# All tensor sums of the MLPs, their norms and V on VectorE instead of GpSimd, with the adds into y between operand splits and four pairs of operands fetched ahead

## The chip, the cores and the metric

The program runs on one core of one Trainium2 chip. The metric is the device time of one execution in microseconds (us), the median of several runs. A core has five engines that run side by side: PE (TensorE: matmuls, with PEld for its weight loads), DVE (VectorE), ACT (ScalarE), POOL (GpSimd) and SP (SyncE, which here only issues transfers). Each engine runs its instructions in the order in which they stand in its own queue, and an instruction that waits for another engine or for a transfer holds up everything behind it in that queue.

## The reference, cut to what matters

A sequence of 1024 tokens of width 1024, float32, goes through a state-space layer (S5), a norm, an MLP, a norm, then attention, a norm, a second MLP and a last norm:

```
for layer in range(2):
    mix = s5_mixer(x, ...) if layer == 0 else attention(x, k, v, ...)
    x  = layer_norm(ALPHA * x + mix, ...)
    h  = square(relu(x @ w1 + b1))          # 1024 -> 4096
    x  = layer_norm(ALPHA * x + h @ w2 + b2, ...)   # 4096 -> 1024
```

Before layer 1 the shared K and V are made from the output of layer 0 (`v = x @ w_v`). float32 matmuls are done with two reduced-precision halves of each operand: a high part (a cast) and a low part (the operand minus its high part); three products (high x high, high x low, low x high) are summed in PSUM.

## The kernel before

Every MLP matrix product uses Strassen's scheme in Winograd's form on 2 x 2 blocks, so seven products M1 to M7 stand in the place of eight. Their operands are sums of blocks of x, w1, h or w2, and their results are added into more than one block of the output.

**Names.** `split` (L121 to L123) makes the two halves of a 128x512 tile: ACT casts the high part (L122), DVE subtracts for the low part (L123). m0 and m1 are the first matrix of the MLP in layers 0 and 1 (`mlp_up`), d0 and d1 the second (class `Down`). In Down, `d0hM`/`d1hM` is a raw tile of h or of a sum of its blocks (made by mlp_up, kept in DRAM as h_d), `w_d0HM`/`w_d1HM` its two halves; `d0r`/`d1r` is a raw block of w2, `w_d02M`/`w_d12M` the halves of a w2 operand; `d0M`/`d1M` is a PSUM tile, `d0y`/`d1y` the output rows.

**Down.** The contraction over 4096 is cut into 16 pairs of blocks p, four pairs to a chunk, so four chunks. In a chunk the products come in the order M1, M2, M5, M6, M3, M7, M4, each as four units, one for each pair. That is 7 x 4 x 4 = 112 units. A unit is 12 matmuls (four token tiles t, three products each; L1070 to L1072), and the four units of a product add up in four PSUM tiles. There are two sets of these: M1, M6, M7 and M4 use set A, M2, M5 and M3 set C. Where M2 is followed by M5, M7 by M4, or M4 by the next chunk's M1, the next product begins in the very tiles that the last one has filled, so PE may start only when `evict` (L1076 to L1079, on DVE) has added them into y.

The raw block of w2 is turned into the next product's operand in place: `prep` (L1041 to L1061) has one sum on POOL for M5 (L1047), M6 (L1050), M7 (L1055) and M4 (L1060), none for M1, M2 and M3, then a split of h's tile and one of w2's. The loop of `run` goes over the units with operands made LA=3 units ahead and h's tiles loaded LH=2 units before that; behind the last unit of a product stand the four evictions. `load_h`, `load_raw` and `load_y` issue their transfers on SP. `ahead` (L1012 to L1030) runs inside mlp_up: it prepares ALPHA * x + b2 in DRAM (ACT scale L1021, POOL add L1022), and loads and splits the first operands of Down.

**Norms.** `LayerNorm` takes the statistics on DVE (L182 to L190), a power on POOL (L192, 128x1), the centring on ACT (L194), the scale by g on DVE (L203) and the addition of b (L204), the last on POOL but for the second half of the last tile. The norms of the first four token tiles of d0 and d1 run while the last products of Down do. `XOps` makes from the normed x the seven operands of mlp_up: sums (L249 to L256, two on DVE, two on POOL, for a pair of token tiles), transposes on PE, splits.

**V.** `VProject.load` loads and splits w_v; the low part is on POOL for the first eight tiles (L1226), on DVE for the others. It begins during the last units of d0.

The order inside each engine's queue is not quite that of the code: a scheduler moves an instruction forward or back where its dependences and its buffers let it.

Of the kernel before, what the change touches and what calls it, by code (L numbers as in the profile page):

```python
# [9 lines left out]
F32 = mybir.dt.float32  # L10
# [6 lines left out]
P = 128  # L17
# [16 lines left out]
CH = 4  # L34
# [11 lines left out]
def trunk(ctx, tc, A, out):  # L46
# [126 lines left out]
    class LayerNorm:  # L173
# [46 lines left out]
    class XOps:  # L220
# [24 lines left out]
        def more(self, tp_, tag):  # L245

            for n_ in ("T2", "T3", "T4"):
                self.op[n_] = self.two(tp_, tag, n_)

        def sums(self, y, t):  # L250
# [4 lines left out]
            pool.tensor_sub(b0, b1, b0)  # L255
            pool.tensor_sub(a1, t2, a1)  # L256

        def second(self, psp, tag, y, t):
            self.put(psp, tag, "T1", y[t - 4][:, half(0)], t)
            self.put(psp, tag, "B22", y[t][:, half(1)], t)  # L260

        def third(self, psp, tag, y, t):
            self.put(psp, tag, "T2", self.t2.pop(t), t)
# [546 lines left out]
    def mlp_up(l, xo, y_tiles, w1, nm, ypool, tpool, tag, wb, uside, rest, down):  # L810
# [24 lines left out]
        ring = tpool.tile([P, 2, 4, HF], F32, tag=tag, name=f"{nm}ring")  # L835
# [31 lines left out]
        early(1)  # L867
        xo.third(psX, "p", y_tiles, 5)
        rest[1]()
# [9 lines left out]
        early(5)  # L879
        xo.second(psX, "p", y_tiles, 7)  # L880
        early(6)
# [44 lines left out]

        def after(p, m):
            if m in ("M1", "M5", "M6"):
                keep(p, m)
            elif m == "M3":  # L930
                dve.tensor_add(h_new(p, "A21"), tmp[p, "M6"], bank(p, m))
                finish(p, "A21", hs[p, "A21"], 1.0, 0)
            elif m == "M7":
                dve.tensor_add(h_new(p, "A22"), tmp[p, "M5"], bank(p, m))
                finish(p, "A22", hs[p, "A22"], -1.0, 1)
                store(p, "A22", 6)
                dve.tensor_add(h_new(p, "s1"), hs[p, "A21"], hs[p, "A22"])
                store(p, "s1", 1)
            elif m == "M2":
                dve.tensor_add(h_new(p, "A11"), tmp[p, "M1"], tmp[p, "M2"] if p < EA else bank(p, m))  # L940
                finish(p, "A11", hs[p, "A11"], 1.0, 0)
                store(p, "A11", 0)
            else:
# [3 lines left out]
                h_new(p, "s2")  # L947
                dve.scalar_tensor_tensor(hs[p, "s2"], hs[p, "s1"], -1.0, hs[p, "A11"], op0=ALU.mult, op1=ALU.subtract)
                store(p, "s2", 2)
                dve.tensor_add(h_new(p, "s3"), hs[p, "A11"], hs[p, "A21"])  # L950
                store(p, "s3", 4)
                dve.tensor_sub(h_new(p, "s4"), hs[p, "A12"], hs[p, "s2"])
                store(p, "s4", 3)
# [639 lines left out]
```

## Time and profile before

| what | value |
|---|---|
| median of 3 runs | 2513.43 us (2513.2 to 2515.7) |
| the profiled execution | 2512.12 us |
| its span, first to last instruction | 2510.4 us |
| mean granted TensorE clock | 0.971 of full speed |
| PE, DVE, ACT, POOL busy | 92%, 73%, 48%, 35% |
| m0, d0, m1, d1 on PE, from the span's start | 483 to 822, 822 to 1166, 1814 to 2151, 2151 to 2490 us |
| last matmul to the end of the span | 20 us |

Times are microseconds unless marked ns. In a group of instructions, "x112" is the count, "| 94.8, 847 |" the busy time and the mean ns of one, and what follows is the idle time of the engine just ahead of them with what ended most of it. In a timeline each row has the start, the duration, the engine, the line and the operation, and in brackets the engine's idle time before it and who ended it. Rows that a timeline has put together ("x4") have the time of all of them. Matmuls overlap: their starts are 0.23 us apart though each lasts 0.39.

### The profile page before, as it was taken

The numbers are of one execution on the slowest core, as the hardware profiler recorded it, in microseconds if no ns is written. First come the engines' busy times: TensorE is split into PE (matmuls) and PEld (weight loads), VectorE is DVE, ScalarE is ACT, GpSimd is POOL, SyncE is SP. The second block draws the span as 40 slices with busy tenths as digits, with TensorE's granted clock in tenths as the row PEclk, the third lists the DMA queues.
The fourth block names the chain that finished last, engine by engine and source line by source line (L and its number), as shares of the span: only waits on it lengthen the run. The fifth ranks groups of instructions, "written<-read, shape, count | busy, mean of one in ns | idle before, by whom it ended". The sixth has DMA issues, their size and how long they took to land. (4 is left out here: it accounts for less than half of the span.)

```text
span 2510.4 us, 32876 instructions
## 1 busy us (share of the span) xinstructions
PE 2306.3 (92%) x11040; PEld 1882.6 (75%) x11040; DVE 1837.8 (73%) x2652; ACT 1214.0 (48%) x2283; POOL 876.5 (35%) x1012
## 2 busy tenths in 40 slices
PE   9886899989999899998999999988989999899995
PEld 7675787767888777776878788766767888777774
DVE  8788573886665687789159999896777665677787
ACT  5445351365555333434147677663356555344333
POOL 5556340552111431136134444340443112422234
PEclk9989999999999999999999999998999999999998
DMA  4221131365443845435565555555366333654432
GB/s 147 55 72 45 35 126 59 136 245 178 155 147 109 274 153 160 143 92 152 107 153 119 122 128 118 118 139 191 122 206 237 141 141 127 235 193 160 129 103 96
DMA packets 195161, 349.39 MB, mean 139 GB/s; under 512 B 23216, under 2 KB 66224, under 8 KB 194992
## 3 DMA queue, kind: packets, MB, share of 16 engines
q1 hardware_dynamic: 136112, 246.61, 31.1%
q0 software_dynamic: 58880, 100.69, 14.5%
q8 instruction: 87, 1.43, 0.2%
q14 instruction: 82, 0.67, 0.1%
HBM read 212.96 MB, written 100.66 MB: 125 GB/s over the span
## 5 line engine op out<-in xcount | busy, mean ns | idle before, releaser
L1070 PE MATMUL d1M<-w_d12M,w_d1HM 128*128 128x512 f32 x448 | 177.2, 397 | 25.8 <-DVE d1y L1079 19.2
L1070 PE MATMUL d0M<-w_d02M,w_d0HM 128*128 128x512 f32 x448 | 177.7, 397 | 21.3 <-DVE d0y L1079 13.3
L1407 DVE TENSOR_TENSOR_SCAN qq<-qq 128x128 f32<-128x128 f32 (+7 forms) x128 | 174.1, 1362 | 11.5 <-POOL qq L1401 11.2
L1072 PE MATMUL d0M<-w_d02M,w_d0HM 128*128 128x512 f32 x448 | 177.2, 396 | 0.0
L1071 PE MATMUL d0M<-w_d02M,w_d0HM 128*128 128x512 f32 x448 | 176.7, 394 | 0.0
L1072 PE MATMUL d1M<-w_d12M,w_d1HM 128*128 128x512 f32 x448 | 176.4, 394 | 0.0
L1071 PE MATMUL d1M<-w_d12M,w_d1HM 128*128 128x512 f32 x448 | 176.3, 394 | 0.0
L122 ACT CAST w_d0HM<-d0hM 128x512 fp32r<-128x512 f32 x112 | 69.5, 620 | 191.4 <-PE d0M L1072 168.6
L122 ACT CAST w_d1HM<-d1hM 128x512 fp32r<-128x512 f32 x112 | 69.5, 620 | 188.8 <-PE d1M L1072 165.1
L123 DVE TENSOR_TENSOR w_d0HM<-d0hM,w_d0HM 128x512 fp32r<-128x512 f32 x112 | 94.8, 847 | 72.3 <-ACT w_d0HM L122 72.2
L123 DVE TENSOR_TENSOR w_d1HM<-d1hM,w_d1HM 128x512 fp32r<-128x512 f32 x112 | 92.8, 829 | 70.5 <-ACT w_d1HM L122 70.4
L122 ACT CAST wTh<-pt 128x512 fp32r<-128x512 f32 (+1 forms) x192 | 88.2, 486 | 81.3 <-PE pt L1420 80.8
L1420 PE MATMUL pt<-ident,be 128*128 128x128 f32 x576 | 91.7, 284 | 34.0 <-DVE wTl L123 25.3
L1070 PEld LDWEIGHTS d1M<-w_d12M,w_d1HM 128*128 128x128 f32 x448 | 85.1, 190 | 48.2 <-ACT w_d12M L122 21.2
L1070 PEld LDWEIGHTS d0M<-w_d02M,w_d0HM 128*128 128x128 f32 x448 | 85.6, 191 | 43.4 <-ACT w_d02M L122 22.9
L1401 POOL TENSOR_SCALAR_AFFINE_SELECT qq<-qq 128x128 f32<-128x128 f32 x128 | 60.2, 470 | 158.9 <-ACT qq L1398 133.4
L1420 PEld LDWEIGHTS pt<-ident,be 128*128 128x128 f32 x576 | 70.7, 144 | 59.8 <-issue 16.4
L123 DVE TENSOR_TENSOR w_d12M<-d1r,w_d12M 128x512 fp32r<-128x512 f32 x112 | 106.1, 948 | 4.2 <-ACT w_d12M L122 4.2
L123 DVE TENSOR_TENSOR wTl<-pt,wTh 128x512 fp32r<-128x512 f32 (+1 forms) x192 | 99.8, 546 | 11.7 <-ACT wTh L122 11.6
L123 DVE TENSOR_TENSOR w_d02M<-d0r,w_d02M 128x512 fp32r<-128x512 f32 x112 | 102.6, 917 | 4.2 <-ACT w_d02M L122 4.2
L1408 DVE TENSOR_TENSOR be<-be,qq 128x127 f32<-128x127 f32 (+7 forms) x128 | 99.5, 778 | 6.6
L1398 ACT ACTIVATE qq<-pz 128x512 f32<-128x512 f32 (+1 forms) x192 | 97.3, 507 | 10.8 <-DVE be L1408 5.9
(468 smaller groups left out, 7398.1 us busy)
## 6 DMA issues: line engine op xcount, KB each, us to landing
d0hM<-h_d SPq DMA_DIRECT2D x112, 256.0 KB, 2.7
d1hM<-h_d SPq DMA_DIRECT2D x112, 256.0 KB, 2.7
m0ring<-in_w SPq DMA_DIRECT2D x64, 256.0 KB, 3.1
h_d<-m0hs POOLq DMA_DIRECT2D x64, 256.0 KB, 2.8
d0r<-in_w SPq DMA_DIRECT2D x64, 256.0 KB, 3.6
m1ring<-in_w SPq DMA_DIRECT2D x64, 256.0 KB, 3.1
h_d<-m1hs POOLq DMA_DIRECT2D x64, 256.0 KB, 2.6
d1r<-in_w SPq DMA_DIRECT2D x64, 256.0 KB, 3.5
```

Of the source, the lines that this page charges most:

```text
L122: act.copy(hi, src)
L123: dve.tensor_sub(lo, src, hi)
L1070: pe.matmul(ps_, hh[:, tok(t)], wh, start=first, stop=False, skip_group_check=True)
L1071: pe.matmul(ps_, hh[:, tok(t)], wl, start=False, stop=False, skip_group_check=True)
L1072: pe.matmul(ps_, hl[:, tok(t)], wh, start=False, stop=last, skip_group_check=True)
L1398: act.activation(qq[:, s0:s1], pz, AF.Sigmoid, scale=-0.125)
L1401: pool.affine_select(out=tl[:, ns - P:ns], in_=tl[:, ns - P:ns], pattern=[[-1, P]], compare_op=ALU.is_gt, fill=fill, base=0, channel_multi ...
L1407: dve.tensor_tensor_scan(out=rev, data0=rev, data1=rev, initial=1.0, op0=ALU.mult, op1=ALU.bypass)
L1408: dve.tensor_mul(be[:, 0:ns - 1], be[:, 0:ns - 1], qq[:, 1:ns])
L1420: pe.transpose(pt[:, b_], self.be[:, tok(s0 + b_)], ident)
```

## The change

1. The sums of w2's blocks in Down, the adds of b2 in `ahead`, the adds of b in the norms, two of the sums in XOps and the low parts of w_v go from POOL to DVE. The power of the norm, the transfers that POOL issues and the selects in the attention stay on POOL.
2. `prep` is cut into `prep_h` and `prep_w`. At the last unit of a product the order becomes: h's split, two evictions, w2's sum and split, two evictions.
3. Down starts with operands fetched earlier: the ring in which mlp_up keeps raw blocks of w1 is now allocated by XOps (T1 takes its old place), and when mlp_up is through with a part of it, `ahead` loads into it the raw blocks and h's tiles of M1 for pairs 2 and 3 and the four blocks of w2 for M2.
4. In mlp_up the sums s1 to s4 that follow a product are put behind the next product; XOps' T1 transposes come later.
5. In layer 0 the norms of token tiles 2 and 3 move from the end of d0 into V.

```diff
@@ LayerNorm.scale
-                (dve if c.start else pool).tensor_add(y[:, c], y[:, c], self.b[:, c])
+                dve.tensor_add(y[:, c], y[:, c], self.b[:, c])
@@ XOps
-            self.op = {n_: self.two(pl, "act", n_) for n_ in ("B11", "B21", "B22", "T1")}
+            self.op = {n_: self.two(pl, "act", n_) for n_ in ("B11", "B21", "B22")}
+            self.ring = pl.tile([P, 2, 4, HF], F32, tag="act", name=f"{nm}ring")
...
-            pool.tensor_sub(b0, b1, b0)
-            pool.tensor_sub(a1, t2, a1)
+            dve.tensor_sub(b0, b1, b0)
+            dve.tensor_sub(a1, t2, a1)
@@ mlp_up
             prod(p, m, ready.pop((p, m)))
+            if later:
+                later.pop(0)()
             if m == "M5" and p < EA:
-                after(p, "M1")
                 after(p, "M2")
-            down.ahead(i, NSTEPS)
+            if m == "M4" and p + 1 < EA:
+                keep(p + 1, "M1")
+            down.ahead(i, NSTEPS, xo.ring)
             if (p, m) == (0, "M3"):
                 continue
-            after(p, m)
+            later += after(p, m)
@@ Down.ahead
-                    pool.tensor_add(self.yt, self.yt, self.b2[:, half(q % 2)])
+                    dve.tensor_add(self.yt, self.yt, self.b2[:, half(q % 2)])
...
+            if i == n - 7:
+                for q, p in enumerate((2, 3)):
+                    self.load_raw(p, [(0, 0)], to=ring[:, 0, 2 * q])
+                    self.load_h(p, "M1", to=ring[:, 0, 2 * q + 1])
             if i == n - 2:
-                self.ready[0, "M1"] = self.prep(0, "M1")
+                for p in range(4):
+                    self.load_raw(p, [(1, 0)], to=ring[:, 1, p])
+            if i == n - 2:
+                self.ready[0, "M1"] = self.prep_h(0, "M1"), self.prep_w(0, "M1")
@@ Down.prep_w
-                pool.tensor_sub(w, w, r(1, 2))
+                dve.tensor_sub(w, w, r(1, 2))
...
-                pool.tensor_sub(w, r(1, 1), w)
+                dve.tensor_sub(w, r(1, 1), w)
@@ Down.run
-            self.load_h(2, "M1")
-            self.load_raw(2, [(0, 0)])
-            self.load_raw(3, [(0, 0)])
+            self.load_h(0, "M2")
             self.load_y(0, 0)
-            for p in range(CH):
-                self.load_raw(p, self.PARTS[1:2])
...
-                        ready[p, m] = self.prep(p, m)
+                        hw.append(self.prep_h(p, m))
+                        if not end:
+                            hw.append(self.prep_w(p, m))
+                            ready[p, m] = hw
...
-                if q == CH - 1:
-                    for t in range(4):
-                        self.evict(m, t)
+                if end:
+                    self.evict(m, 0)
+                    self.evict(m, 1)
+                    if hw:
+                        c, m_, p = units[i + LA]
+                        hw.append(self.prep_w(p, m_))
+                        ready[p, m_] = hw
...
+                    self.evict(m, 2)
+                    self.evict(m, 3)
@@ VProject.load
-            act.copy(t[:, 0], r)
-            eng.tensor_sub(t[:, 1], r, t[:, 0])
+            split(t[:, 0], t[:, 1], r)
```

In the program as built, 216 tensor sums leave POOL's queue: 128 of w2, 32 of b2, 32 of the norms' b, 16 of XOps and 8 of w_v. PE's and ACT's queues keep their lengths.

The first place is VectorE in d0, second chunk, around the end of M2, where M5 begins in the same PSUM tiles. Before, `w_d0HM` and `w_d02M` are the low halves of operands, and L1079 is the eviction; the sums of w2 stand in POOL's queue:

```order
L123 TENSOR_TENSOR w_d0HM_7635<-d0hM_7587,w_d0HM_7635 128x512
L123 TENSOR_TENSOR w_d02M_7638<-d0r_7353,w_d02M_7638 128x512
L123 TENSOR_TENSOR w_d0HM_7656<-d0hM_7611,w_d0HM_7656 128x512
L123 TENSOR_TENSOR w_d02M_7659<-d0r_7382,w_d02M_7659 128x512
L1079 TENSOR_TENSOR d0y_6781<-d0y_6781,d0M_7595 128x512
L1079 TENSOR_TENSOR d0y_6782<-d0y_6782,d0M_7596 128x512
L1079 TENSOR_TENSOR d0y_6783<-d0y_6783,d0M_7597 128x512
L1079 TENSOR_TENSOR d0y_6784<-d0y_6784,d0M_7598 128x512
L123 TENSOR_TENSOR w_d0HM_7681<-d0hM_7632,w_d0HM_7681 128x512
L123 TENSOR_TENSOR w_d02M_7684<-d0r_7415,w_d02M_7684 128x512
```

Now, at the same place (L1105 is the eviction, L1082 the sum for M6 and L1086 that for M4):

```order
L123 TENSOR_TENSOR w_d0HM_7626<-d0hM_7579,w_d0HM_7626 128x512
L123 TENSOR_TENSOR w_d02M_7630<-d0r_7345,w_d02M_7630 128x512
L1082 TENSOR_TENSOR d0r_7345<-d0r_7345,d0r_7351 128x512
L1086 TENSOR_TENSOR d0r_7347<-d0r_7345,d0r_7347 128x512
L123 TENSOR_TENSOR w_d0HM_7647<-d0hM_7603,w_d0HM_7647 128x512
L1105 TENSOR_TENSOR d0y_6789<-d0y_6789,d0M_7587 128x512
L1105 TENSOR_TENSOR d0y_6790<-d0y_6790,d0M_7588 128x512
L123 TENSOR_TENSOR w_d02M_7665<-d0r_7388,w_d02M_7665 128x512
L1105 TENSOR_TENSOR d0y_6791<-d0y_6791,d0M_7589 128x512
L1105 TENSOR_TENSOR d0y_6792<-d0y_6792,d0M_7590 128x512
L123 TENSOR_TENSOR w_d0HM_7672<-d0hM_7624,w_d0HM_7672 128x512
L123 TENSOR_TENSOR w_d02M_7676<-d0r_7407,w_d02M_7676 128x512
```

Two evictions now stand ahead of the last low half of w2, and two behind it. The sums of M6 and M4 stand behind the last split that reads the block they overwrite, four units or more ahead of the product that uses them; the scheduler has put them there.

The second place is SP's queue where d0 begins. Before, the raw blocks of w1 go to `m0ring`, `r_v` belongs to V, `d0y` is the output's rows:

```order
L842 DMA m0ring<-in_w 128x512 x40
L1223 DMA r_v_9460<-in_w_kv 128x512
L1223 DMA r_v_9465<-in_w_kv 128x512
L1223 DMA r_v_9470<-in_w_kv 128x512
L1038 DMA d0hM_6789<-h_d 128x512
L1083 DMA d0y_6781<-xm_d 128x512
L1083 DMA d0y_6782<-xm_d 128x512
L1083 DMA d0y_6783<-xm_d 128x512
L1083 DMA d0y_6784<-xm_d 128x512
L1038 DMA d0hM_6807<-h_d 128x512
L1038 DMA d0hM_6815<-h_d 128x512
L1038 DMA d0hM_6823<-h_d 128x512
```

and ten loads of `d0r` at L1034 follow. Now the ring is `x1ring`, and L1065 and L1069 are the loads of w2's blocks and of h's tiles:

```order
L843 DMA x1ring<-in_w 128x512 x37
L1065 DMA x1ring<-in_w 128x512 x2
L1069 DMA x1ring<-h_d 128x512 x2
L1065 DMA x1ring<-in_w 128x512 x2
L1259 DMA r_v_9412<-in_w_kv 128x512
L1259 DMA r_v_9417<-in_w_kv 128x512
L1259 DMA r_v_9422<-in_w_kv 128x512
L1065 DMA x1ring<-in_w 128x512 x2
L1069 DMA d0hM_6797<-h_d 128x512
L1109 DMA d0y_6789<-xm_d 128x512
L1109 DMA d0y_6790<-xm_d 128x512
L1109 DMA d0y_6791<-xm_d 128x512
```

Eight of the loads that stood behind y's four rows now stand ahead of them, six of w2's and two of h's.

## Rows read from the trace of the kernel before

**Rows 1.** The page's first part: busy time, share of the span and number of instructions.

```profile
PE 2306.3 (92%) x11040; PEld 1882.6 (75%) x11040; DVE 1837.8 (73%) x2652; ACT 1214.0 (48%) x2283; POOL 876.5 (35%) x1012
```

**Rows 2.** The page's costliest groups: the first matmul of each three in d1 and d0, with PE's idle time before them, and the low halves of w2's operands.

```profile
L1070 PE MATMUL d1M<-w_d12M,w_d1HM 128*128 128x512 f32 x448 | 177.2, 397 | 25.8 <-DVE d1y L1079 19.2
L1070 PE MATMUL d0M<-w_d02M,w_d0HM 128*128 128x512 f32 x448 | 177.7, 397 | 21.3 <-DVE d0y L1079 13.3
...
L123 DVE TENSOR_TENSOR w_d12M<-d1r,w_d12M 128x512 fp32r<-128x512 f32 x112 | 106.1, 948 | 4.2 <-ACT w_d12M L122 4.2
...
L123 DVE TENSOR_TENSOR w_d02M<-d0r,w_d02M 128x512 fp32r<-128x512 f32 x112 | 102.6, 917 | 4.2 <-ACT w_d02M L122 4.2
```

**Rows 3.** PE's waits in d0 (822 to 1166 us): who waited for whom, us in total, times, the longest.

```profile
PE d0M L1070 <- DVE d0y L1079: 13.3, 7, 2.0
PE d0M L1070 <- ACT w_d02M L122: 8.0, 2, 6.7
PE ptd L211 <- POOL d0y L204: 4.5, 3, 1.9
```

and in d1 (2151 to 2490 us):

```profile
PE d1M L1070 <- DVE d1y L1079: 19.2, 8, 6.1
PE d1M L1070 <- ACT w_d12M L122: 6.6, 1, 6.6
```

**Rows 4.** The timeline of d0 around 909 us, where M2 of the first chunk ends and M5 begins in its tiles: DVE and POOL, and the two matmuls on either side of PE's gap. The first row is an operation that no POOL sum overlaps; PE begins M2's last unit at 906.6, 12 matmuls ahead of 909.4.

```profile
902.67 0.69 DVE L123 TENSOR_TENSOR w_d02M<-d0r,w_d02M 128x512 fp32r<-128x512 f32 x1
...
906.85 0.62 ACT L122 CAST w_d0HM<-d0hM 128x512 fp32r<-128x512 f32 x1 [1.58 <-PE d0M L1072]
...
907.50 1.58 DVE L123 TENSOR_TENSOR w_d0HM<-d0hM,w_d0HM 128x512 fp32r<-128x512 f32 x1 [0.33 <-ACT w_d0HM L122]
908.61 1.60 POOL L1055 TENSOR_TENSOR d0r<-d0r,d0r 128x512 f32<-128x512 f32 x1
909.01 1.76 DVE L123 TENSOR_TENSOR w_d02M<-d0r,w_d02M 128x512 fp32r<-128x512 f32 x1
...
910.69 2.47 DVE L1079 TENSOR_TENSOR d0y<-d0y,d0M 128x512 f32<-128x512 f32 x4
...
909.14 0.39 PE L1072 MATMUL d0M<-w_d02M,w_d0HM 128*128 128x512 f32 x1
911.51 0.47 PE L1070 MATMUL d0M<-w_d02M,w_d0HM 128*128 128x512 f32 x1 [1.98 <-DVE d0y L1079]
```

**Rows 5.** Groups of d0's whole stretch (822 to 1166 us): the slowest and the fastest kind of the POOL sums of w2.

```profile
L1060 POOL TENSOR_TENSOR d0r<-d0r,d0r 128x512 f32<-128x512 f32 x16 | 25.3, 1580 | 1.1
...
L1047 POOL TENSOR_TENSOR d0r<-d0r,d0r 128x512 f32<-128x512 f32 x16 | 20.5, 1285 | 142.3 <-DVE w_d02M L123 129.8 <-DMA d0r<-in_w 12.5
```

**Rows 6.** The start of d1: SP's queue, the first cast that had waited for its block, and the matmuls on either side of the gap; the last row is from the chain of waits, the transfer that released the cast.

```profile
2154.23 9.26 SPq L1034 DMA_DIRECT2D d1r<-in_w  x10
...
2162.49 0.62 ACT L122 CAST w_d12M<-d1r 128x512 fp32r<-128x512 f32 x1 [0.81 <-DMA d1r<-in_w]
...
2156.20 0.39 PE L1072 MATMUL d1M<-w_d12M,w_d1HM 128*128 128x512 f32 x1
2163.16 0.80 PE L1070 MATMUL d1M<-w_d12M,w_d1HM 128*128 128x512 f32 x1 [6.57 <-ACT w_d12M L122]
...
2154.23 8.23 DMA d1r<-in_w
```

**Rows 7.** The end of d1, from M7 to M4: POOL, DVE and the matmuls on either side of the gap.

```profile
2467.76 2.92 POOL L204 TENSOR_TENSOR d1y<-d1y,d1b 128x1024 f32<-128x1024 f32 x1 [2.09 <-DVE ved L189]
...
2468.32 2.91 DVE L123 TENSOR_TENSOR w_d12M<-d1r,w_d12M 128x512 fp32r<-128x512 f32 x1
...
2470.72 0.39 PE L1072 MATMUL d1M<-w_d12M,w_d1HM 128*128 128x512 f32 x1
2477.18 0.76 PE L1070 MATMUL d1M<-w_d12M,w_d1HM 128*128 128x512 f32 x1 [6.07 <-DVE d1y L1079]
```

**Rows 8.** The tail of d1, DVE and POOL, from the last evictions to the last addition.

```profile
2487.61 1.29 DVE L1079 TENSOR_TENSOR d1y<-d1y,d1M 128x512 f32<-128x512 f32 x2 [1.50 <-PE d1M L1072]
...
2493.62 3.44 POOL L204 TENSOR_TENSOR d1y<-d1y,d1b 128x1024 f32<-128x1024 f32 x1 [1.33 <-DVE ved L189]
...
2497.02 0.54 POOL L192 TENSOR_TENSOR rsd<-ved,nhalf 128x1 f32<-128x1 f32 x1
...
2497.60 3.35 DVE L203 SCALAR_TENSOR_TENSOR d1y<-d1y,rsd,d1g 128x1024 f32<-128x1024 f32 x1 [2.14 <-POOL rsd L192]
...
2505.36 1.63 DVE L204 TENSOR_TENSOR d1y<-d1y,d1b 128x512 f32<-128x512 f32 x1
```

**Rows 9.** PE's waits in layer 0's projection (381 to 483 us), in V (1166 to 1263 us) and in m1 (1814 to 2151 us), one row of each view.

```profile
PE ptx1T L237 <- DVE y L252: 3.9, 1, 3.9
...
PE pv L118 <- POOL w_v L1226: 1.8, 2, 1.0
...
PE m1A L830 <- DVE m1hA L934: 2.5, 2, 1.6
```

**Rows 10.** Two stretches of the timeline: layer 0's projection (POOL's adds of b beside DVE's splits), and a sum of mlp_up in layer 1.

```profile
468.83 6.13 POOL L204 TENSOR_TENSOR y<-y,sob 128x1024 f32<-128x1024 f32 x2 [1.51 <-DVE y L203]
...
469.86 6.24 DVE L123 TENSOR_TENSOR w_m<-r_m,w_m 128x512 fp32r<-128x512 f32 x3
...
1872.88 3.43 DVE L940 TENSOR_TENSOR m1hA<-m1kM,m1kM 128x512 f32<-128x512 f32 x1
```

More of the change, by code (lines that the diff above doesn't have):

```diff
@@ L867, in mlp_up @@
         early(1)
+        rest[1]()
         xo.third(psX, "p", y_tiles, 5)
-        rest[1]()
         early(2)
@@ L925, in store, with add @@
             pool.dma_start(h_d[p, q], hs[p, n_])
+        def add(p, n_, a, b, op=ALU.add):
+            dve.tensor_tensor(h_new(p, n_), a, b, op=op)
         def after(p, m):
+            later = []
             if m in ("M1", "M5", "M6"):
@@ L957, in mlp_up @@
         steps += [(p, m) for p in range(EA, NP) for m in PROD]
-        ready = {}
+        ready, later = {}, []
         LA = 2
         NSTEPS = len(steps)
+        keep(0, "M1")
         for i in range(-LA, NSTEPS):
@@ L1128, in run @@
             for i in range(-LA, N):
-                if 0 <= i + LA + LH < N and i + LA + LH > 2:
+                if 0 <= i + LA + LH < N and i + LA + LH > CH:
                     self.load_h(units[i + LA + LH][2], units[i + LA + LH][1])
+                end = i >= 0 and units[i][2] % CH == CH - 1
+                hw = []
                 if i + LA < N:
@@ L1133, in run @@
                     if (p, m) not in ready:
-                        ready[p, m] = self.prep(p, m)
-                    if m == "M4" and c + 1 < NP // CH:
+                        hw.append(self.prep_h(p, m))
+                        if not end:
+                            hw.append(self.prep_w(p, m))
+                            ready[p, m] = hw
+                    if m == "M4" and c + 1 < NP // CH and not end:
                         self.load_raw(p + CH, self.PARTS)
@@ L1141, in run @@
                     for _ in range(2):
-                        then.load(0, then.wv, pool)
+                        then.load(0, then.wv)
                 if i < 0:
@@ L1170, in run @@
                             self.unit(p_, m_, ops, (t,), f_, l_)
-                        for f, a in queue.pop(0) if queue else ():
-                            f(a)
                         self.evict(m, t)
@@ L1189, in run @@
                 if fin and m == "M7" and q == CH - 1:
-                    for t in range(4, 8):
+                    for t in range(2 if then else 4, 8):
                         ln(t)
@@ L1195, in run @@
                 for k in range(KD):
-                    then.load(0, then.wv, pool)
+                    then.load(0, then.wv)
                 then.xa = xn
@@ L1216, in begin, with load @@
             self.ws = [[], []]
-        def load(self, n, pl, eng):
+        def load(self, n, pl):
             k = len(self.ws[n])
@@ L1239, in mm @@
                 self.out(n, t, pv)
+            for t in (2, 3):
+                lns[t].stats()
+                lns[t].center()
+            for t in (2, 3):
+                lns[t].scale()
             for t in range(8):
@@ L1245, in run @@
                     lns[4 + t].center()
-                if 1 <= t < 5:
-                    lns[3 + t].scale()
-                if 2 <= t < 6:
+                if t < 6:
+                    if t > 1:
+                        lns[2 + t].scale()
                     trans(t + 2)
-                self.load(1, sl.next(), dve)
+                self.load(1, sl.next())
             for t in range(8):
```

88 lines of the change are left out of this document (48 added, 40 removed).

## The prediction, made before the changed kernel had run

> **What bounds the kernel now.** I read the page's first part, then its costliest groups, PE's waits stage by stage, and timelines of the places where PE stood still. PE is busy for 92% of the span [rows 1], so no edit off PE's path is worth anything, and the most that can be had is PE's idle time. The reader should look at the matmul groups: nearly all of it in the two second MLP matrices stands ahead of the first matmul of a triple, L1070, 25.8 us in d1 and 21.3 in d0 [rows 2]. The waits say for whom: VectorE's evictions, 19.2 and 13.3 us, and the cast of a w2 operand, 6.6 and 8.0 us, nearly all of these in one wait in each layer [rows 3]. So two kinds of wait hold most of what this change could win in Down.
>
> The first is seen around 909 us [rows 4]. M2's last unit starts at 906.6, and its first PSUM tile is complete three matmuls later, at about 907.3. Yet the four evictions start at 910.69, because VectorE is still at two splits of 1.58 and 1.76 us. The same operation takes 0.69 with no GpSimd sum beside it. PE's starts are 2.37 apart there, less a pitch of 0.23, so 2.14 us is lost. The second is a transfer: ten loads of w2 need 9.26 us to be issued, the one that is wanted lands 8.23 us after its issue, and PE's starts at 2156.20 and 2163.16 are 6.96 apart, 6.73 lost [rows 6].
>
> **The change part by part.** The profiled execution took 2512.1 us, 1.3 less than the median; sums are made against it.
>
> *Start of Down.* The operands of M1's four units and the w2 blocks of M2 are fetched inside mlp_up, and eight loads leave the queue ahead of PE's first wants. Nothing that PE needs in the first eight units then waits for the stretch of saturated loads, apart from M2's h tiles. One such gap measures 6.73 [rows 6], the other's wait is as long, 6.7 against 6.6 [rows 3]; after it matmuls take 0.80 in place of 0.39 for a while [rows 6], half a microsecond or so. Both layers: 14 at most. I take -13; if y's rows and h's tiles in the same queue keep half of it, -6; if the queue merely moves the wait to M5, -4.
>
> *Evictions.* d0 has seven waits, d1 seven of the same kind and the 6.1 us one near its end [rows 3]. By 2.14 each, the first of a layer being shorter by some 0.6, that is 14.4 a layer, 28.8 in all. What takes their place? Four evictions back to back take 2.47, one 0.69, so VectorE's pitch is (2.47 - 0.69) / 3 = 0.59, say 0.60 [rows 4]. Count from the start of the last unit: the cast of h starts 0.2 later (906.85 against 906.6) [rows 4], the low half is possible when it ends, at 0.86 and ends its slot at 1.46. The first two evictions then go, done at 2.15 and 2.75, w2's low half has its slot to 3.26, and the other two are done at 3.95 and 4.55. PE wants the four tiles at 2.74, 3.42, 4.10 and 4.79. So nothing waits, but with a margin of 0.15 to 0.7 us only. Left over I put 4 us, for places where VectorE arrives late by a few tenths (14 places by 0.3). Value -24; ends -28.8, and -10 where the last two evictions are late at every place by one slot or more.
>
> This needs VectorE to be on time in spite of its new work: 64 w2 sums a layer. They take GpSimd 1.29 to 1.58 each [rows 5]; VectorE has them for one slot, 0.60. The order places sums for two products behind the splits of M1 and of M5, so these phases hold 8 splits, 8 sums and 4 evictions: 20 x 0.60 = 12.0 against PE's 4 x 2.74 = 10.9. The other five phases hold 12 x 0.60 = 7.2. VectorE falls 1.1 behind twice a chunk, with operands three units ahead, and recovers in the next phase. The stretched splits pay for the rest: their means of 948 and 917 ns against 0.69 [rows 2, 4] are 0.24 x 224 = 54 us that w2's splits alone give back, against 128 x 0.60 = 77 for the sums. The first cover is therefore the lead of three units; if it is gone, each sum costs PE up to 0.60.
>
> *End of d0 and V.* PE waits 4.5 us for GpSimd's adds of b ahead of transposes [rows 3] and 1.8 for w_v's low halves [rows 9], 6.3 together. VectorE takes the adds (two slots each, about 1.2, in place of 2.4 to 2.9), and two of the four norms leave for V, where transposes have to wait for them instead. I take -3; ends -6 (all gone) and +4 (VectorE holds four adds, w_v's splits and V's own splits, 8 x 0.6 more, in one queue).
>
> *End of d1 and the tail.* Between M7 and M4 PE loses 6.2 us (2470.72 to 2477.18) [rows 7]: GpSimd's add takes 2.92 and a split beside it 2.91, where both alone would need 0.69 + 1.2. I count 3.5 left, since the splits and the norms still share VectorE: -2.7. In the tail, an add of 3.44 stands ahead of the power that VectorE then waits for, and VectorE's scale takes 3.35 in place of about 1.3 [rows 8]; but the adds now stand in VectorE's own queue, four of 1.2. From first eviction to last add is 2505.36 + 1.63 - 2487.61 = 19.4 us; I reckon 17, of which 1.2 is lost again because PE ends nearer to the evictions. Together -4; ends -8 and +3.
>
> *Projections and mlp_up.* The longest wait at either projection is 3.9 us for the first sum of XOps [rows 9], itself behind three splits of 6.24 in all that run beside two adds of 6.13 [rows 10]. Alone they would be 1.9 and 2.5. Against that, all four sums of a pair and T1 to T4's transposes hang on VectorE, and 16 adds of b2 a layer (9.6 us) land in a queue whose entries wait in order for their loads. Sums of mlp_up that reach 3.43 beside such an add [rows 10] fall to 0.69. Value -3; ends -14 and +10, as no row shows VectorE with this load at this place.
>
> Sum: -13 - 24 - 3 - 4 - 3 = -47, so 2465 for the profiled execution, **2466 us** against the median.
>
> The trace's slot of 0.60 carries the whole reckoning of VectorE. The Trainium skill (VectorE: DVE Perf Modes, "The TRN2 errata") gives an fp32 add of N elements (N + 151) / 0.96 ns, 691 ns for 512, which agrees with the 0.69 of a single one [rows 4] but not with the slot. By it, if an operation held the engine for all of that, 20 in a phase would need 13.8 against 10.9, and sixteen such phases would be 46 us late, an estimate that leaves 2511. The four evictions in 2.47 speak against it.
>
> **The rivals.**
> 1. *VectorE becomes the bound in M1's and M5's phases, or the last two evictions are late.* For: the surplus of 1.1 us and the margin of 0.15. Against: the five light phases, and a lead of three units. If the lead covers nothing, 1.1 x 2 x 8 chunks = 17 us come back: 2483.
> 2. *The start of Down is only half cured.* For: y's four rows and h's tiles are still issued there, at over 9 us for ten loads [rows 6]. Against: M1 needs none of them. 7 us come back: 2473.
> 3. *Slower.* The sums enter PE's path: at the operands where a sum, a cast and a low half follow each other in one unit, VectorE's chain is 0.60 + 0.66 + 0.60 and two more slots for h and an eviction, over 2.74. Every sum then costs PE 0.60, 128 x 0.60 = 77 us, which against the gains of 47 gives 2543. Decides from the point at which VectorE needs over 2.74 for a unit with nothing in hand. For: VectorE is at 73% already [rows 1]. Against: the order puts each sum a product ahead of its use.
> 4. *No effect.* The waits removed are made up by the next ones on PE, such as the casts' transfers, and the time stays at 2513. Against: the gaps are PE's own, and PE has 92% to do.
>
> **How the numbers follow.** Forecast 0.60; first rival 0.20, second 0.11, third 0.04, fourth 0.02; 0.03 for a gain beyond the terms. The forecast's own range, from the ends that are likely at once, is 2452 to 2477. The range that should hold 8 in 10 takes in the first two rivals: 2450 to 2488. A measurement of this kernel tells about 0.2% from no change, 5 us. Faster: forecast, the gain beyond it, both first rivals, and 0.01 kept off for their tails, 0.93. Same 0.03: the fourth rival and a third one that just balances. Slower 0.04.
>
> **What would show it.** Right: in d0 and d1 the waits of PE for the eviction fall from 13.3 and 19.2 to under 5 us each; no gap over 2 us within Down's first eight units; the low halves of w2's operands near 0.69 us on average; VectorE's busy share at 75 to 79%, GpSimd's below 25%, with no sum of w2 on it. Between M7 and M4 of d1 a gap of 3 to 4 us; from the first of the last evictions to the last add 16 to 18 us. Wrong: PE's waits move to the low half of a w2 or h operand on VectorE (rival 1 or 3), to a transfer of y or h in the first 30 us of d0 and d1 (rival 2), or mlp_up gets longer by more than 5 us because VectorE's queue waits there for x's rows.

## The result and the profile after

The changed kernel takes **2423.62 us** (2421.34 to 2428.5) against 2513.31, a ratio of 0.9644 [0.9626, 0.9662]; timed again in five rounds beside two experiments 0.9662 [0.9649, 0.9674]. It is 85 to 90 us faster, nearly twice the 47 forecast and outside the range of 2450 to 2488. The ratios of the experiments below are to the kernel before too, timed in turn with it, and their costs are taken against the 0.9662; 0.001 is 2.5 us. Against the first 0.9644 each cost would read 4.5 us more, so a cost of a few us cannot be told from nothing.

The page's first part after the change, then its groups of L1070's successor:

```profile
span 2419.6 us, 32714 instructions
PE 2274.4 (94%) x11040; PEld 1860.3 (77%) x11040; DVE 1842.8 (76%) x2868; ACT 1211.6 (50%) x2283; POOL 540.0 (22%) x796
...
L1096 PE MATMUL d1M<-w_d12M,w_d1HM 128*128 128x512 f32 x448 | 174.9, 391 | 3.9 <-DVE d1y L1105 3.9
L1096 PE MATMUL d0M<-w_d02M,w_d0HM 128*128 128x512 f32 x448 | 174.6, 390 | 1.6 <-ACT w_d02M L122 1.2
```

The idle times of 25.8 and 21.3 us [rows 2] are 3.9 and 1.6. But look at PE's busy time first: the same 11040 matmuls took 2306.3 us [rows 1] and now take 2274.4, **31.9 us** less, without one of them being changed. The span fell by 90.8, so PE's idle time fell by 58.9. The 31.9 was hardly in the forecast; some of it is scatter between executions, as the account of the clock below shows.

VectorE's busy time is what it was, 1842.8 against 1837.8, although it has 216 more instructions: what the splits no longer lose beside GpSimd pays for the sums. The mean low half of w2 shows it (groups of d0, 807 to 1116 us), with the timeline of a switch below it, from M4 of d0's first chunk to M1 of its second:

```profile
L123 DVE TENSOR_TENSOR w_d02M<-d0r,w_d02M 128x512 fp32r<-128x512 f32 x96 | 65.8, 685 | 0.0
```

```profile
883.85 0.69 DVE L123 TENSOR_TENSOR w_d0HM<-d0hM,w_d0HM 128x512 fp32r<-128x512 f32 x1
884.46 1.28 DVE L1105 TENSOR_TENSOR d0y<-d0y,d0M 128x512 f32<-128x512 f32 x2
885.65 0.68 DVE L123 TENSOR_TENSOR w_d02M<-d0r,w_d02M 128x512 fp32r<-128x512 f32 x1
886.25 1.28 DVE L1105 TENSOR_TENSOR d0y<-d0y,d0M 128x512 f32<-128x512 f32 x2
```

685 ns against 917 [rows 2]; two evictions in 1.28 leave a slot of 0.60, and PE does not stop here at all. VectorE's order is the one that was counted out, with the same 0.60 between starts. It is also the switch of [rows 4], whose evictions at 910.69 are the seventh set of d0 and so M4's of the first chunk; the label M2 to M5, there and in the prediction, is wrong. The prediction's sum does not suffer by it: in the kernel before, a switch from M2 to M5 (PE goes on at 935.50) shows the same 2.37 us between PE's starts as this one (911.51). The Trainium skill (VectorE: DVE Perf Modes, "The TRN2 errata") has 691 ns for an fp32 add of 512 elements; that is about its duration here, 0.68 to 0.69 us, not the time after which the next may start.

Where the time went is seen in a table by stage. Each line has the stretch, its length, then the busy time of PE, PEld, DVE, ACT and POOL with their instructions, the granted clock, the DMA share and GB/s. Before, in the order projection 0, m0, d0, V, projection 1 (with attention's end), m1, d1:

```profile
381.60:482.90 101.30, 96.82 (x433) 78.27 (x433) 55.71 (x85) 22.97 (x33) 24.41 (x16) 0.98 0.25 82
482.90:821.50 338.60, 327.48 (x1411) 260.84 (x1410) 223.10 (x321) 194.43 (x327) 93.45 (x133) 0.98 0.48 169
821.50:1165.50 344.00, 318.16 (x1377) 258.64 (x1376) 266.80 (x368) 137.37 (x238) 113.52 (x81) 0.98 0.50 157
1165.50:1262.60 97.10, 95.31 (x418) 76.51 (x417) 39.03 (x60) 26.33 (x44) 30.98 (x27) 0.98 0.63 141
1647.70:1813.90 166.20, 143.71 (x703) 115.46 (x701) 129.38 (x184) 71.36 (x149) 51.56 (x61) 0.93 0.48 149
1813.90:2151.00 337.10, 324.69 (x1412) 260.56 (x1411) 223.40 (x321) 194.11 (x327) 92.31 (x133) 0.99 0.46 168
2151.00:2490.40 339.40, 313.54 (x1345) 253.81 (x1343) 265.78 (x365) 130.97 (x226) 110.37 (x77) 0.98 0.49 157
```

and after:

```profile
380.40:478.10 97.70, 96.13 (x441) 77.92 (x441) 56.95 (x92) 22.87 (x33) 3.28 (x6) 1.00 0.24 84
478.10:807.20 329.10, 322.73 (x1403) 256.96 (x1401) 224.23 (x349) 195.39 (x330) 59.18 (x110) 1.00 0.52 180
807.20:1116.40 309.20, 307.58 (x1361) 253.01 (x1360) 258.67 (x421) 130.57 (x228) 4.63 (x8) 1.00 0.52 164
1116.40:1213.10 96.70, 95.66 (x433) 76.67 (x432) 48.80 (x84) 30.97 (x51) 17.36 (x20) 1.00 0.67 156
1596.40:1756.00 159.60, 139.41 (x696) 109.99 (x694) 127.00 (x186) 69.97 (x146) 31.50 (x51) 0.97 0.48 148
1756.00:2088.30 332.30, 322.85 (x1420) 260.92 (x1418) 227.77 (x355) 196.04 (x332) 59.12 (x110) 0.99 0.50 179
2088.30:2400.30 312.00, 307.92 (x1345) 251.27 (x1343) 260.97 (x425) 129.16 (x223) 7.67 (x9) 1.00 0.52 163
```

Take d1: 27.4 us shorter. PE's idle time (length less busy) goes from 25.9 to 4.1, and the same 1345 matmuls take 5.6 us less; their clock was 0.98 and is 1.00. d0 is 34.8 shorter, 24.2 of it idle time; 16 transposes (2.1 us of PE's time) have left it for V, which is none the longer, and some 8.5 is clock. The two projections and mlp_up, from which 3 was hoped, are 24.5 shorter: idle time falls from 50.5 to 37.6, busy time by 11.6 with 3960 matmuls in place of 3959. All the rest gave some 4 us. One long wait is new, where m1 begins, for the low halves of x on VectorE:

```profile
PE m1B L832 <- DVE x3T L123: 5.8, 1, 5.8
```

### The profile page after: what moved, and what is told of

The parts are those of the page before. It is cut to its first block, busy times and chain, and to the rows that moved or that the text cites. A ratio compares the mean times of both kernels' runs of the same rounds, so it can differ in the third digit from the quotient of the medians.

```text
span 2419.6 us, 32714 instructions
## 1 busy us (share of the span) xinstructions
PE 2274.4 (94%) x11040; PEld 1860.3 (77%) x11040; DVE 1842.8 (76%) x2868; ACT 1211.6 (50%) x2283; POOL 540.0 (22%) x796
## 4 chain that ended last, share of the span: by engine, by line
PE 64%; DVE 12%; issue 5%; DMA 4%; POOL 2%; ACT 2%; SPq 0%; POOLq 0%; DVEq 0%; ACTq 0%
PE d0M L1096 4%; PE d0M L1097 4%; PE d0M L1098 4%; PE d1M L1096 4%; PE d1M L1098 4%; PE d1M L1097 4%; DVE qq L1447 2%; PE m1A L832 2%; PE m1A L834 2%; PE m1A L833 2%; PE m0A L832 2%; PE m0A L833 2%; PE m0A L834 2%; DVE be L1448 2%; PE po L1474 1%
## 5 line engine op out<-in xcount | busy, mean ns | idle before, releaser
L1096 PE MATMUL d0M<-w_d02M,w_d0HM 128*128 128x512 f32 x448 | 174.6, 390 | 1.6 <-ACT w_d02M L122 1.2
L1097 PE MATMUL d0M<-w_d02M,w_d0HM 128*128 128x512 f32 x448 | 174.5, 389 | 0.0
L1098 PE MATMUL d0M<-w_d02M,w_d0HM 128*128 128x512 f32 x448 | 174.3, 389 | 0.0
L192 POOL TENSOR_TENSOR rsd<-ved,nhalf 128x1 f32<-128x1 f32 x16 | 16.2, 1014 | 621.5 <-DVE ved L190 613.3
L1460 PE MATMUL pt<-ident,be 128*128 128x128 f32 x576 | 90.5, 281 | 34.8 <-DVE wTl L123 25.8
L1460 PEld LDWEIGHTS pt<-ident,be 128*128 128x128 f32 x576 | 69.7, 143 | 60.9 <-issue 18.5
L123 DVE TENSOR_TENSOR w_d1HM<-d1hM,w_d1HM 128x512 fp32r<-128x512 f32 x110 | 75.9, 690 | 52.4 <-ACT w_d1HM L122 52.2
L123 DVE TENSOR_TENSOR w_d0HM<-d0hM,w_d0HM 128x512 fp32r<-128x512 f32 x110 | 75.9, 690 | 51.6 <-ACT w_d0HM L122 51.5
L1096 PEld LDWEIGHTS d1M<-w_d12M,w_d1HM 128*128 128x128 f32 x448 | 84.1, 188 | 24.1 <-ACT w_d12M L122 4.3
L1098 PEld LDWEIGHTS d1M<-w_d12M,w_d1HM 128*128 128x128 f32 x448 | 84.1, 188 | 18.4
L1097 PEld LDWEIGHTS d1M<-w_d12M,w_d1HM 128*128 128x128 f32 x448 | 84.1, 188 | 17.8
```

The source lines that it names most:

```text
L123: dve.tensor_sub(lo, src, hi)
L1096: pe.matmul(ps_, hh[:, tok(t)], wh, start=first, stop=False, skip_group_check=True)
L1097: pe.matmul(ps_, hh[:, tok(t)], wl, start=False, stop=False, skip_group_check=True)
L1098: pe.matmul(ps_, hl[:, tok(t)], wh, start=False, stop=last, skip_group_check=True)
L1460: pe.transpose(pt[:, b_], self.be[:, tok(s0 + b_)], ident)
```

## The experiments

**One part undone at a time.** Down's sums back on GpSimd:

```diff
-                dve.tensor_sub(w, w, r(1, 2))
+                pool.tensor_sub(w, w, r(1, 2))
...
-                dve.tensor_sub(w, r(1, 1), w)
+                pool.tensor_sub(w, r(1, 1), w)
```

> The changed kernel with one thing undone: Down's 128 sums of w2 stand on GpSimd again; the split evictions and the early fetches stay. Theory (a GpSimd sum stretches VectorE's low halves from 0.69 to 1.6 or 1.8 us, and it was this that made the evictions late): at the same-bank switches the low half of h now ends 0.9 us late and the first eviction about 0.4 us after PE wants it, the third about 1.3 after, so some 1.2 us at each of 14 switches and a little more near the end of d1: 15 to 35 us slower than the changed kernel, PE's wait for the eviction 6 to 12 us a layer. Rival (the place of the evictions alone cured it): within 5 us of the changed kernel.

Measured 0.9736 [0.9707, 0.9766], 19 us slower than the changed kernel: the theory. PE's waits in d0 and d1, then VectorE's groups in d0:

```profile
PE d0M L1096 <- DVE d0y L1105: 6.0, 8, 2.1
PE d1M L1096 <- DVE d1y L1105: 8.8, 9, 2.9
```

```profile
L123 DVE TENSOR_TENSOR w_d02M<-d0r,w_d02M 128x512 fp32r<-128x512 f32 x96 | 85.3, 888 | 0.0
L1105 DVE TENSOR_TENSOR d0y<-d0y,d0M 128x512 f32<-128x512 f32 x111 | 70.8, 679 | 0.0
```

The low halves, which read two tiles of SBUF, are stretched to 888 ns; the evictions, which read one of SBUF and one of PSUM, are not, at 679. The Trainium skill (SBUF — State Buffer, "Who interferes with whom") says that a VectorE instruction with two SBUF inputs contends with a GpSimd one that reads SBUF; these rows agree.

The evictions together again, with the sums on VectorE:

```diff
-                    self.evict(m, 0)
-                    self.evict(m, 1)
...
-                    self.evict(m, 2)
-                    self.evict(m, 3)
+                    for t in range(4):
+                        self.evict(m, t)
```

> The changed kernel with one thing undone: the four evictions stand together behind both splits again; the sums stay on VectorE. Theory (VectorE's slots of 0.60 count and nothing else): h's low half ends its slot 1.46 us into the last unit, w2's at 2.06, the four evictions are done at 2.75, 3.35, 3.95 and 4.55 against 2.74, 3.42, 4.10 and 4.79: 0 to 5 us slower than the changed kernel. Rival (the evictions between the splits are what removed the waits): 2.1 us at 14 switches come back, 25 to 35 us slower.

0.9679 [0.9654, 0.9703], 4 us slower, which the intervals do not part from nothing, nor from some 10 us. The rival's 25 to 35 us are out. So of the two things done for the evictions it was the freed splits that counted; what the new places are worth while the sums stand on GpSimd was not run.

The loads at the start of Down as before:

```diff
-            if i == n - 7:
-                for q, p in enumerate((2, 3)):
...
-                for p in range(4):
-                    self.load_raw(p, [(1, 0)], to=ring[:, 1, p])
...
+            for p in range(CH):
+                self.load_raw(p, self.PARTS[1:2])
...
```

> The changed kernel with one thing undone: pairs 2 and 3 of M1 and the four blocks of M2 are loaded at the start of Down again. Theory: PE's wait of 6.6 us for a cast returns in both layers, and behind it the granted clock stands at its lower level for some us, which costs about half of them: 2 x (6.7 + 2 to 3.4) = 17 to 20 us slower. Rival one (the sums on GpSimd took part in that wait): under 10 us. Rival two (no clock effect): 13 to 14 us.

0.9738 [0.9711, 0.9765], 19 us slower, as the theory has it. In its profile d0 and d1 together are 16.0 us longer than in the changed kernel's, and 4.9 of that is PE's busy time; the timing alone, with its interval, would not rule out the 13 to 14 us of rival two. PE's waits at their start are back, though GpSimd has no sum there:

```profile
PE d0M L1088 <- ACT w_d02M L122: 7.1, 1, 7.1
PE d1M L1088 <- ACT w_d12M L122: 6.8, 1, 6.8
```

The adds of the norms, of b2 and of XOps on GpSimd again (80 sums):

```diff
-                dve.tensor_add(y[:, c], y[:, c], self.b[:, c])
+                (dve if c.start else pool).tensor_add(y[:, c], y[:, c], self.b[:, c])
...
-                    dve.tensor_add(self.yt, self.yt, self.b2[:, half(q % 2)])
+                    pool.tensor_add(self.yt, self.yt, self.b2[:, half(q % 2)])
```

> The changed kernel with one group undone: the adds of b in the norms, of b2 ahead of Down and the two XOps sums stand on GpSimd again (80 sums); w2's sums and w_v stay on VectorE, mlp_up's later sums stay. Theory (the 24 us won in the projections and mlp_up, where 3 were forecast, are waits behind operations stretched by these GpSimd adds, and the lower clock behind those waits): 15 to 28 us slower, most of it in the projections and the first 90 us of m0 and m1. Rival (the new order of mlp_up's sums won them): under 6 us slower there.

0.9779 [0.9751, 0.9807], 29 us slower, a little over the theory's upper end; m0 and m1 are 343 and 342 us long, 14 and 10 more. Then the 32 adds of b2 alone:

> The changed kernel with only the 32 adds of b2 ahead of Down on GpSimd again (16 a layer, all within the first 90 us of m0 and m1); the norms' adds and XOps' sums stay on VectorE. Theory (stretching by the adds of b2 is the larger part of what m0 and m1 lost before, since they fall where mlp_up's own sums are dense): 12 to 25 us slower than the changed kernel, in m0 and m1. Rival (the norms' adds of 2.4 to 3.4 us and XOps did it): under 8 us slower.

0.9738 [0.9719, 0.9758], 19 us, in the theory's range and two thirds of the whole group's cost. m0 and m1:

```profile
478.10:818.30 340.20, 327.59 (x1403) 260.01 (x1401) 229.49 (x333) 196.38 (x330) 82.51 (x126) 0.98 0.51 174
1764.20:2109.30 345.10, 327.46 (x1420) 263.01 (x1419) 231.38 (x339) 197.04 (x332) 81.30 (x126) 0.98 0.49 173
```

m0 has idle time of 12.6 in place of 6.4 and 4.9 us more for the same 1403 matmuls. One place where PE waits, in the timeline of VectorE, GpSimd and PE:

```profile
532.91 3.27 DVE L123 TENSOR_TENSOR w_m01M<-m0sM,w_m01M 128x512 fp32r<-128x512 f32 x1
...
533.13 2.50 POOL L1044 TENSOR_TENSOR d0ya<-d0ya,d0b 128x512 f32<-128x512 f32 x2
...
536.24 0.51 PE L834 MATMUL m0A<-x1T,w_m01M 128*128 128x512 f32 x1 [2.46 <-DVE w_m01M L123]
```

A low half lasts 3.27 us, through two adds, and PE waits 2.46 for it.

**One part done alone**, in the kernel before: the same 80 sums to VectorE and nothing else.

> The kernel before with one part of the change done alone: the adds of b in the norms, of b2, and XOps' two sums go from GpSimd to VectorE (80 sums); w2's sums, the evictions, the fetches and w_v stay as before. Theory (the groups act on different stages and add up): 18 to 30 us faster than before, all of it outside the middle of Down, with Down's waits for the evictions unchanged at 13 us a layer. Rival (VectorE only pays off when all of GpSimd's sums are gone, or the new order of mlp_up is needed as well): under 8 us faster.

0.9894 [0.9875, 0.9913], 27 us faster than before, as the theory says. m0 and m1 are 333.8 and 334.0 us long, d1 is unchanged at 339.8, and in Down the waits for the evictions stay:

```profile
PE d0M L1070 <- DVE d0y L1079: 15.3, 8, 2.1
```

So most of what the projections and mlp_up gave, 18.5 us of the 24.5, comes without anything new in Down. d0 is 5.6 shorter as well, since PE's wait for the adds of b ahead of the transposes at its end falls from 4.5 [rows 3] to 0.7. The order of mlp_up's sums has no part that shows: put back, it changed nothing that can be told from the scatter.

```diff
-            if later:
-                later.pop(0)()
...
-            later += after(p, m)
+            for f in after(p, m):
+                f()
```

> The changed kernel with mlp_up's loop in its old order: the sums s1 to s4 directly behind their product, the copy of M1 where it was; everything else, the adds on VectorE too, as in the changed kernel. Theory (mlp_up gained from VectorE being free of GpSimd's adds, not from the order of its sums): within 6 us of the changed kernel's 2423. Rival (the deferred sums keep VectorE free for the next operand): m0 and m1 each 5 us or more longer, 10 to 20 us slower in all.

> The kernel e5_sums_at_once once more, since the profile of its first run shows a granted clock of 0.65 through the whole span and says nothing on stages. Theory (the order of mlp_up's sums is worth little): m0 and m1 together at most 6 us longer than in the changed kernel, the whole within 6 us. Rival (the deferred sums matter): m0 and m1 together 10 to 20 us longer.

0.9671 [0.9646, 0.9696] and, repeated, 0.9657 [0.9644, 0.9669] beside the unaltered changed kernel's 0.9662: the theory. m0 and m1 are 332.2 and 333.4 long in that repetition, against 329.4 and 333.1 in the changed kernel timed beside it.

> The changed kernel, unaltered, beside the two that follow, on the same chip: the ratio to the kernel before should be the 0.9644 of its first timing, within 0.003, whatever the theory.

It was 0.9662, 0.0018 above.

**Stretch, or waiting for GpSimd's result?** b2's adds on GpSimd could also have cost because y and GpSimd's queue wait for them. Three kernels add 32 GpSimd sums that nobody needs and leave the real adds on VectorE:

```diff
+                    pool.tensor_add(junk, self.b2[:, half(0)], self.b2[:, half(1)])
```

> The changed kernel with 32 added GpSimd sums that nothing needs (16 a layer, 128x512, the two halves of b2 into a scratch tile), next to the adds of b2, which stay on VectorE. No GpSimd instruction waits for a load or a scale that it did not wait for before, and nothing that PE needs comes out of the added sums. Theory (a GpSimd sum costs because VectorE's operations beside it are stretched, in the part of m0 and m1 where they are dense): 8 to 20 us slower than the changed kernel, with operations of 1.3 to 3.4 us on VectorE in m0's first 90 us. Rival (what cost was the dependence: GpSimd's queue, with the stores of h, waiting for the adds' loads and scales, and y waiting for GpSimd): under 5 us slower.

0.9672 [0.9655, 0.9689], 2.5 us, which the intervals do not part from nothing: the rival's number, but not a test. The scratch tiles came from a shared pool and held the sums back (count, shortest, median and longest in ns, first and last start; e6's real adds first, this one's second):

```profile
L1044 POOL TENSOR_TENSOR d0ya<-d0ya,d0b x16: 1259/1362/1807, 509.8 to 562.7; 128x512 f32<-128x512 f32 x16
```

```profile
L1046 POOL TENSOR_TENSOR d0jk<-d0b x16: 1288/1292/3492, 551.3 to 744.2; 128x512 f32<-128x512 f32 x16
```

They met VectorE where it has time: in the changed kernel it is busy for 65% of 551 to 744 us, and for 84% of 505 to 565. With a scratch tile of its own, and each sum reading the tile that VectorE has just finished (`pool.tensor_add(self.junk, self.yt, ...)`), the place is right:

```profile
L1047 POOL TENSOR_TENSOR d0jk<-d0ya,d0b x16: 1272/1606/2811, 515.7 to 575.0; 128x512 f32<-128x512 f32 x16
```

> The changed kernel with 32 added GpSimd sums that nothing needs, this time in the place that matters: each reads the tile to which VectorE has just added b2, and writes a scratch tile of its own, so they fall into the first 90 us of m0 and m1 as the adds of b2 do. VectorE keeps its own adds. Theory (VectorE's operations are stretched beside a GpSimd sum where mlp_up's are dense): 12 to 25 us slower than the changed kernel, in m0 and m1, as with the adds themselves on GpSimd. Rival (the cost was that y's rows and mlp_up waited for GpSimd's result): under 5 us slower, since nothing waits for these results but the buffers they read.

0.9738 [0.9724, 0.9753]: 19 us, the very cost of the real adds, from sums whose results nobody reads. It is the stretch. VectorE is busy for 76.7 of the 80 us from 500 to 580, against 66.9 in the changed kernel, and no engine waits for the added sums. Nor does VectorE wait there for the stores of h, which GpSimd issues in the same queue. m0's waits for VectorE's own work:

```profile
PE m0A L832 <- DVE m0hA L929: 6.0, 4, 2.0
PE m0A L834 <- DVE w_m01M L123: 1.7, 1, 1.7
```

The same number of sums, reading nothing but b2, stand in a clump in each layer; here is the first:

```profile
L1047 POOL TENSOR_TENSOR d0jk<-d0b x16: 1285/1604/1637, 512.2 to 537.8; 128x512 f32<-128x512 f32 x16
```

> The changed kernel with 32 added GpSimd sums that depend on nothing but b2 (into the same scratch tile), so that they stand in two clumps of 16 ahead of the adds of b2, about 20 us of unbroken GpSimd work where m0 and m1 begin. Theory (stretch): 5 to 15 us slower, less than where the sums are spread over mlp_up's dense 50 us, as a clump of 20 us meets fewer of VectorE's operations. Rival (dependence): under 3 us slower.

0.9779 [0.9763, 0.9795], 29 us. The direction was the theory's, the size was not: an unbroken clump costs more, not less. VectorE cannot catch up between sums: from 512.2 to 539.0 us it is busy without a break and does 18 operations, where the changed kernel does 38 in the same stretch. Behind it PE waits 6.8 us for a single sum of h:

```profile
PE m0A L832 <- DVE m0hA L929: 7.2, 2, 6.8
```

**What a stand costs beyond itself.** In the changed kernel, reads of a PSUM tile ahead of an eviction make PE stand.

```diff
+                    for _ in range(late):
+                        dve.tensor_tensor(junk, self.bank(m, 0), self.y[0][:, half(0)], op=ALU.max)
```

> The changed kernel with reads of a PSUM tile added on VectorE ahead of the first eviction at nine same-bank switches in the middle of Down (3, 5, 7 and 10 reads in d0; 14, 4, 6, 8 and 12 in d1), so that PE stands still for about 1 to 8 us at each; the values read go to a scratch tile that nothing uses. It measures what a stand of PE costs beyond its own length. Theory (behind the longer stands the granted clock is at its lower level for some us, and PE's starts are then 0.43 apart in place of 0.23): stands of up to 2 us cost only themselves nearly always, those of 4 us and more 1.5 to 3.5 us beyond. Rival (the stand alone costs): nothing beyond 0.5 us at any of the nine.

Only three of the nine made a stand of 2 us or more, of 7.0, 5.1 and 2.7 us; the others VectorE absorbed. The matmuls on either side of the longest and the shortest of the three, then stretches behind all three (the fourth-last number is the granted clock):

```profile
2183.63 0.39 PE L1098 MATMUL d1M<-w_d12M,w_d1HM 128*128 128x512 f32 x1
2190.83 0.80 PE L1096 MATMUL d1M<-w_d12M,w_d1HM 128*128 128x512 f32 x1 [6.82 <-DVE d1y L1105]
...
1049.74 0.39 PE L1098 MATMUL d0M<-w_d02M,w_d0HM 128*128 128x512 f32 x1
1052.62 0.50 PE L1096 MATMUL d0M<-w_d02M,w_d0HM 128*128 128x512 f32 x1 [2.49 <-DVE d0y L1105]
```

```profile
2188.00:2194.80 6.80, 3.97 (x9) 3.14 (x10) 4.97 (x9) 2.14 (x4) 0.00 (x0) 0.50 0.00 0
2351.80:2358.60 6.80, 5.21 (x12) 4.13 (x13) 5.61 (x10) 3.24 (x6) 0.00 (x0) 0.50 0.15 36
1052.50:1060.00 7.50, 7.38 (x32) 6.12 (x33) 7.29 (x13) 4.37 (x8) 0.00 (x0) 1.00 0.52 143
```

Behind the stands of 7.0 and 5.1 us the clock is at its lower level, 1.2 GHz, and 9 matmuls take 3.97 and 12 take 5.21, where 0.228 each would be 2.1 and 2.7: 1.9 and 2.5 us on top. Behind the stand of 2.7 the clock stays at 1.00. That is the theory for long stands, on three samples; none of the nine made a stand of 1 to 2 us. Between the two the outcome is mixed: a stand of 3.1 us at the end of d1 is followed by a clock of 0.54 in this run (2416.4 to 2420.0 us), the same stand in the changed kernel by 1.00 (2388.8 to 2392.5). The kernel before shows both kinds. Its rows are the stretch behind the stand of 6.8 us where d0 begins, the stretch behind one of d0's stands of 2.1 us, and d1 from 2168 to 2474 us, where there are seven stands of 1.4 to 2.1 us and the clock does not fall:

```profile
833.84:839.40 5.56, 5.55 (x12) 4.08 (x13) 3.69 (x6) 2.55 (x5) 1.95 (x2) 0.50 1.05 391
993.00:996.40 3.40, 3.40 (x10) 2.67 (x9) 2.57 (x4) 0.00 (x0) 2.09 (x3) 0.51 0.14 28
2168.00:2474.00 306.00, 289.95 (x1261) 235.66 (x1259) 244.78 (x332) 122.86 (x213) 97.21 (x67) 1.00 0.48 151
```

**An attempt to go further.** ALPHA x + b2 in one VectorE operation:

```diff
-                    act.activation(self.yt, self.yt, AF.Copy, scale=ALPHA)
-                    dve.tensor_add(self.yt, self.yt, self.b2[:, half(q % 2)])
+                    dve.scalar_tensor_tensor(self.yt, self.yt, ALPHA, self.b2[:, half(q % 2)], op0=ALU.mult, op1=ALU.add)
```

> The changed kernel with the preparation of ALPHA x + b2 as one VectorE operation in place of a scale on ScalarE and an add on VectorE (32 scales fewer in all, the same number of VectorE operations). Theory (what is left of m0's and m1's early waits hangs on ScalarE's copies and on VectorE's queue waiting for the scale): 1 to 8 us faster than the changed kernel. Rival (those waits come from VectorE's own load, which stays the same): within 2 us.

0.9658 [0.9646, 0.9671]: no difference, the rival. No version tried beats the changed kernel by more than the scatter.

Undone one at a time, the three parts that count cost 19 (Down's sums), 19 (the loads) and 29 us (the other 80 sums), 67 of the 85. The eight sums of w_v and the two norms moved into V were not undone, and how the parts act together was not run.

## Why the prediction was wrong, point by point

*What bounds it, and the direction*: right. PE's idle time ahead of L1070 was the thing to win, and nearly all of it in Down was won.

All the signs that the prediction named for being right came out. But nearly all of them are signs of Down, and the two steps that failed lie outside them.

*Start of Down, -13*: right but for the clock. The 6.7 us gaps are gone, e3 brings both back, and 19 us with them.

*Evictions, -24 with 4 left over*: right, and the leftover smaller: 0.4 us of PE's wait in d0, in d1 1.0 beside the last switch, which has 2.9:

```profile
PE d0M L1096 <- DVE d0y L1105: 0.4, 1, 0.4
PE d1M L1096 <- DVE d1y L1105: 3.9, 3, 2.9
```

Rival 1, VectorE as the bound, did not happen, and the estimate from the Trainium skill's 691 ns (VectorE: DVE Perf Modes, "The TRN2 errata") fell with it. The cause was right (e1), while the split of the evictions, on which much of the working went, measured 4 us (e2), no clear gain.

*End of d0 and V, -3; end of d1 and tail, -4*: nearly right. d0 has no wait at its end. In d1 the wait from M7 to M4 is 2.9 us, and PE loses 3.1 between starts, against a gap of 3 to 4 forecast, and the tail from the first eviction to the last add is 2414.57 + 1.29 - 2398.92 = 16.9 against 17:

```profile
2398.92 0.68 DVE L1105 TENSOR_TENSOR d1y<-d1y,d1M 128x512 f32<-128x512 f32 x1
...
2414.57 1.29 DVE L204 TENSOR_TENSOR d1y<-d1y,d1b 128x512 f32<-128x512 f32 x2
```

Down, V and the tail were forecast at -44 together, of which 1 was clock. They gave 63: 16 of clock, and 47 of idle time and tail. The idle time was thus forecast within a tenth.

*Projections and mlp_up, -3*: the first step that failed. It gave 24.5, outside the ends of -14 and +10 that it was given; 12.9 of it is idle time. The forecast saw operations of 3.43 and 2.08 us [rows 10], but set their relief against VectorE's 16 extra slots as if both were paid in the same coin. The slots fell into time that VectorE had; the stretches stood in front of PE. e6 and e12 price 32 such GpSimd sums at 19 us, 0.6 each, while as many where VectorE has time cost 2.5 or nothing (e10).

*The clock*: the second, and larger. The forecast took "half a microsecond or so" behind the two longest gaps, though its own rows showed matmuls of 0.80 and 0.76 us there [rows 6, 7] and the page a clock of 0.971. In place of 1 us the profiles show 31.9: 16 in Down and V, 11.6 in the projections and mlp_up, 4 elsewhere. The last 4 lie in stretches that the change does not touch and are scatter: a second profile of the changed kernel has PE busy for 2279.2, 27.1 less than before. The mean granted clock was 0.9706 over 38 timed executions of the kernel before and 0.980 over 8 of the changed one; (1 - 0.9706) x 2510 = 73.8 us lost against (1 - 0.980) x 2425 = 48.5 is 25 less. So the clock gave 25 to 32 us, and the profiled pair is a lucky one for it. e8 shows the mechanism and its size per stand; that the whole is answered by particular stands that went was not shown one by one.

With 46 of the forecast's 47 as idle time, about 13 of the 44 us that it missed in the profiled pair is idle time and about 31 is clock. The result lies where the prediction had left 0.03, a gain beyond its terms. None of the four rivals came true; against the third, slower, it had set that each sum stands a product ahead of its use, and PE waits for no sum and no low half in d0 and d1.

## What to carry to other kernels

A long wait of the matmul engine can cost more than its length (1.9 and 2.5 us more in e8): read the granted clock and the duration of the matmuls behind each long wait, and add what the slow stretch costs. A change of PE's total busy time at an equal number of matmuls shows the whole of it, but take more than one profile of each kernel: two of the changed kernel differ in it by 4.8 us. An elementwise sum on GpSimd is paid twice, in GpSimd's own time and in that of every VectorE operation beside it that reads two tiles of SBUF, so it is nearly free only where VectorE has slack; a sum moved to VectorE costs one slot there, 0.60 us here. Weigh such a move by where the stretched operations stand, not by comparing busy times.

## What was not expected of the hardware

In the kernel before, one of the fourteen stands of 1.4 to 2.1 us at evictions was followed by the lower clock and thirteen were not, while each of the stands of 5 us and more shown here was; stands of about 3 us went either way, and what decides was not looked for. A clump of GpSimd sums cost half as much again as the same number spread out (29 against 19 us). And VectorE ran 216 more instructions in about the same busy time, 1842.8 us against 1837.8.
